# Cross-covariance attention: two heads per gram product, fp32 transposes into the gram banks, 512-byte buffers and a new order

## The chip, the cores and the metric

The kernel runs on one NeuronCore of one Trainium2 chip. The metric is the device time of one execution in microseconds (us). Three timed executions of the kernel before gave 131.87, 131.96 and 134.25 us, median 131.96. One further execution was profiled; all durations below are from that one. The engines are named as the profile names them: PE is the matrix engine (PEld its weight loads), DVE the vector engine, ACT the scalar engine, POOL the GpSimd engine, SP the engine that issues nearly all DMAs.

## The reference

Eight batches of twelve heads, 96 heads in all, each with Q, K and V of 512 x 64 in fp32. The attention is between the 64 channels, not between the 512 positions:

```python
Q_norm = Q / (np.linalg.norm(Q, axis=-2, keepdims=True) + 1e-10)
K_norm = K / (np.linalg.norm(K, axis=-2, keepdims=True) + 1e-10)
attn = np.einsum('bhnd,bhne->bhde', Q_norm, K_norm)
attn = np.exp(attn - np.max(attn, axis=-1, keepdims=True))
attn = attn / (np.sum(attn, axis=-1, keepdims=True) + 1e-10)
return np.einsum('bhnd,bhde->bhne', V, attn)
```

Each of Q, K, V and the output is 12.58 MB, so 37.75 MB are read and 12.58 MB written.

## The kernel before, in words

The 96 heads are worked in S = 12 units of eight heads: four partition groups of 32 (h), and in each two heads (r). Two neighbouring units share one V block (w, six of them), which comes as two loads. For each unit s:

- `load_qk` (line 215) loads Q and K, 1 MB each, into one of six buffers; units named in `FINE` (0 and 1) load in halves of 512 KB. `load_v` (231) loads V into one of three buffers.
- `cast_k` (246) and `mask_q` (251) cast K and Q to bf16 (through the helper `copy`, lines 209, 211 and 213 for ACT, DVE and POOL). `square` (263) squares them: on DVE from the bf16 tile (271), on ACT from the fp32 tile (268).
- `grams` (273, product in line 282) forms K^T Q. One product takes one head and two of its time slices t, t+1 side by side, so the two 64x64 diagonal blocks of its 128x128 result are two halves of one head's gram, still to be added; a unit has 64 of them, with 32 partitions each. They land in a PSUM tile of four banks, one bank for each h.
- `sums` (291, line 297) adds the squares over partitions, eight products in a unit; `fold` (300) reduces the rest on DVE; `norms` (304, line 307) brings the sums onto partitions with two products, one for the upper and one for the lower 64 partitions; `powers` (309) makes 1/norm by Ln and Exp on ACT.
- `scale_k` (315, line 319) multiplies the gram by K's factors, in two DVE operations on 64 partitions each. `logits` (325, line 327) multiplies the scaled gram with `eye2`, two identities stacked: that adds the two halves and transposes at once; an fp32 product is two instructions in the trace, so eight for a unit. It writes to the bank `l` (pool `ps_l`, one buffer) that sums and norms use too.
- `scales_q` (329, line 331), `exps` (333), `normalise` (337; z in line 339, rinv 341, rb 343, ab 346) finish the softmax; the result `ab` is block-diagonal bf16 for two heads.
- `cast_v` writes V as bf16 pairs, `vtrans` (359) transposes them on PE, `vcopy` brings them to SBUF as `vt`, `outs` (374) multiplies with `ab` into `po`, `ocopy` copies `po` to `so`, and `store` (235) writes 1 MB. Unit S - 3 is stored in four pieces by partitions (`CUTS`, line 240).

Each of these is a piece of work with a guessed cost for each engine that may do it, the pieces that it must follow (`after`), the pieces that it may not overtake (`behind`) and a rank. A planner, `Order.run` (100), places the pieces in a model of the engines, one at a time, and the kernel is then emitted in that order: each engine has a fixed list, and SP's list of loads and stores is fixed as well. For casts, squares, V casts and the two kinds of copies (`CHOICE`, 434) the planner also picks the engine: the one with the lowest model end plus a `BIAS` for that kind and engine. `R` holds the ranks. `NB` has the numbers of buffers. What holds a buffer back is in lines 451 to 482: a Q or K load waits for the cast and the square of the unit that had the buffer (`uses`, 452); `gr` waits for both `kx` of the unit before (478); `s1` waits for `qs` of the unit before (481).

SBUF tiles are allotted in the order in which their pools are opened. The pool `const` is opened first, with two tiles `front0` and `front1` of 64 bytes that nothing uses; from the sizes of its tiles, the Q/K buffers and all large buffers behind them start 448 bytes past a multiple of 512.

Of the kernel before, what the change touches and what calls it, by code (L numbers as in the profile page):

```python
# [13 lines left out]
PAR = {'NB': {'qk': 6, 'v': 3, 'vb': 2, 'qm': 3, 'sq': 1, 'vt': 2, 'so': 7, 'sm': 2, 'ab': 4},  # L14
 'TAIL': 3,
 'FINE': (0, 1),
 'LONG': (),
 'BOTH': 4,
 'ACTQ': True,
 'X': 1.27,  # L20
 'R': {'ck': 1.3207,
       'q': 6.2518,
       'sq': -0.5047,
       'sk': 3.7122,
       'gr': 1.845,
       's1': -1.9166,
       'rd': -3.4497,
       'nn': 4.2104,
       'pw': -2.4263,
       'kx': 0.7415,  # L30
       'lg': -4.357,
       'qs': 2.8064,
       'ex': -3.2847,
       'nm': 0.8664,
       'cv': 1.7734,
       'vt': -1.4345,
       'vc': 8.5873,
       'ou': 6.3652,
       'oc': 0.5305},
 'BIAS': {('cv', 'DVE'): 1.4481,  # L40
          ('vc', 'ACT'): 0.7387,
          ('oc', 'DVE'): 0.1673,
          ('q0', 'ACT'): -2.0331,
          ('sk', 'ACT'): 0.1695,
          ('ck', 'DVE'): -0.7752,
          ('ck', 'ACT'): 3.4068,
          ('ck', 'POOL'): 0.1916,
          ('q0', 'DVE'): 1.3494,
          ('q0', 'POOL'): 1.3168,
          ('sq', 'DVE'): 0.5356,  # L50
          ('sq', 'ACT'): 0.3766,
          ('sk', 'DVE'): -1.1633,
          ('cv', 'ACT'): -0.4971,
          ('cv', 'POOL'): 0.2974,
          ('vc', 'DVE'): 0.9359,
          ('oc', 'ACT'): -0.8803},
 'QK_PACE': 1.1686,
 'V_FROM': 0.1368,
 'V_PACE': 1.8786,
 'ST_LAG': 2.2074,  # L60
# [11 lines left out]
class Order:  # L72
    HOP = 0.10
# [78 lines left out]
def kernel(  # L152
# [13 lines left out]
    FINE, LONG = PAR["FINE"], PAR["LONG"]  # L166
    BOTH = S - PAR["BOTH"]

    Qf, Kf = (x.rearrange("b h (p t) d -> (b h p) (t d)", t=TT).rearrange("(w r e p) x -> w e p r x", r=2, e=2, p=128)
              for x in (Q, K))  # L170
    Qs, Ks = (x.rearrange("b h (p t) d -> (b h p) (t d)", t=T).rearrange("(w r e p) x -> w e p r x", r=2, e=2, p=64)
# [7 lines left out]
    const = ctx.enter_context(tc.tile_pool(name="const", bufs=1))  # L179
# [7 lines left out]
    abp = ctx.enter_context(tc.tile_pool(name="abp", bufs=NB["ab"]))  # L187
    small = ctx.enter_context(tc.tile_pool(name="small", bufs=NB["sm"]))
# [13 lines left out]
    qk32, kb, qm, sq, v32, vb, gram, st, s2, nn, r12, kqs, lg, ls, ex, ab, vps, vt, po, so = ({} for _ in range(20))  # L202
# [12 lines left out]
    def load_qk(s, x, c):  # L215
        w, e = divmod(s, 2)
        if (s, x) not in qk32:
            qk32[s, x] = qp.tile([128, T, D], F32, name="qk32")
        issue = nc.scalar if (s, x) == (0, 1) and PAR["ACTQ"] else nc.sync
        o = qk32[s, x][:, cols(c)].rearrange("p t d -> p (t d)")  # L220
        if s not in LONG:
            i = (Qf, Kf)[x][w, e]
            if c is None:
                issue.dma_start(out=o.rearrange("p (r x) -> p r x", r=2), in_=i)
            else:
                issue.dma_start(out=o, in_=i[:, c])
            return
        for r in range(2):
            issue.dma_start(out=o[r::2], in_=(Qs, Ks)[x][w, e, :, r, cols(c).start * D:cols(c).stop * D])
# [16 lines left out]
    def cast_k(eng, s, c):  # L246
        if s not in kb:
            kb[s] = qmp.tile([128, T, D], BF16, name="kb")
        copy(eng, kb[s][:, cols(c)], qk32[s, 1][:, cols(c)])

    def mask_q(eng, s, n, c):
        if s not in qm:
            qm[s] = qmp.tile([128, 2, T, D] if s in LONG else [128, T, D], BF16, name="qm")
        if s not in LONG:
            copy(eng, qm[s][:, cols(c)], qk32[s, 0][:, cols(c)])
            return
        o, i, m = qm[s][:, n, cols(c)], qk32[s, 0][:, cols(c)], par[:, n:n + 1]
        if eng == "ACT":
            nc.scalar.activation(o, i, AF.Copy, scale=m)
        else:  # L260
            (nc.vector if eng == "DVE" else nc.gpsimd).tensor_scalar(out=o, in0=i, scalar1=m, scalar2=0.0, op0=ALU.mult, op1=ALU.add)

    def square(eng, s, x, c):
        if s not in sq:
            sq[s] = sqp.tile([128, 2, T, D], BF16, name="sq")
        o = sq[s][:, x, cols(c)]
        if eng == "ACT":
            nc.scalar.activation(o, qk32[s, x][:, cols(c)], AF.Square)  # L268
        else:
            i = (kb if x else qm)[s][:, cols(c)]  # L270
            nc.vector.tensor_tensor(out=o, in0=i, in1=i, op=ALU.mult)  # L271

    def grams(s, c):
        if s not in gram:
            gram[s] = ps_g.tile([128, HU, 2, 2, 2 * D], F32, name="gram")
        if s not in LONG:
            for r in range(2) if c is None else (c,):
                for t in range(0, TT, 2):
                    for h in range(HU):
                        p = slice(32 * h, 32 * (h + 1))  # L280
                        k, q = (y[s][p, TT * r + t:TT * r + t + 2].rearrange("p t d -> p (t d)") for y in (kb, qm))
                        nc.tensor.matmul(gram[s][:, h, 0, r], k, q, start=(t == 0), stop=(t == TT - 2))  # L282
            return
        for t in range(cols(c).start, cols(c).stop, 2):
            for h in range(HU):
                p = slice(32 * h, 32 * (h + 1))
                nc.tensor.matmul(gram[s][:, h, 0].rearrange("p r d -> p (r d)"),
                                 kb[s][p, t:t + 2].rearrange("p t d -> p (t d)"),
                                 qm[s][p, :, t:t + 2].rearrange("p r t d -> p r (t d)"), start=(t == 0), stop=(t == T - 2))

    def sums(s, c):
        if s not in st:
            st[s] = ps_l.tile([D, 8, D], F32, name="l")
        for t in range(cols(c).start, cols(c).stop, 8):
            for x in range(2):
                m = hm[:, 0] if s in LONG else hm[:, 1 + t // TT]
                nc.tensor.matmul(st[s][32 * x:32 * (x + 1)].rearrange("p t d -> p (t d)"), m,  # L297
                                 sq[s][:, x, t:t + 8].rearrange("p t d -> p (t d)"), start=(t == 0), stop=(t == T - 8))

    def fold(s):  # L300
        s2[s] = small.tile([D, D], F32, name="s2")
        nc.vector.tensor_reduce(out=s2[s], in_=st[s].rearrange("p t d -> p d t"), axis=mybir.AxisListType.X, op=ALU.add)  # L302

    def norms(s):
        nn[s] = ps_l.tile([128, 12], F32, name="l")
        for i, half in enumerate((LO, HI)):
            nc.tensor.matmul(nn[s][half], s2[s], sel[:, i], start=True, stop=True)

    def powers(s):
        ln = small.tile([128, 12], F32, name="ln")  # L310
        r12[s] = small.tile([128, 12], F32, name="r12")
# [3 lines left out]
    def scale_k(s, n):  # L315
        if n == 0:
            kqs[s] = small.tile([128, 2 * HU, D], F32, name="kqs")
        half = (LO, HI)[n]
        nc.vector.tensor_tensor(  # L319
            out=kqs[s][half].rearrange("p (h r) d -> p h r d", r=2), in0=gram[s][half, :, 0, :, half],  # L320
            in1=r12[s][half, 0:2 * HU].rearrange("p (h r) -> p h r", r=2)[:, :, :, None].to_broadcast([D, HU, 2, D]), op=ALU.mult,
        )

    def logits(s):
        l = lg[s] = ps_l.tile([128, HU, D], F32, name="l")
        for h in range(HU):
            nc.tensor.matmul(l[:, h, :], kqs[s][:, 2 * h:2 * h + 2].rearrange("p r d -> p (r d)"), eye2, start=True, stop=True)  # L327

    def scales_q(s):
        ls[s] = small.tile([128, HU, D], F32, name="ls")  # L330
        nc.vector.tensor_tensor(out=ls[s], in0=lg[s], in1=r12[s][:, 8:12, None].to_broadcast([128, HU, D]), op=ALU.mult)  # L331
# [50 lines left out]
    pads = [const.tile([128, D // 4], F32, name=f"front{i}") for i in range(2)]  # L382
# [12 lines left out]
    par = const.tile([128, 2], F32, name="par")  # L395
    nc.vector.tensor_reduce(out=par, in_=ident.rearrange("p (i r) -> p r i", r=2), axis=mybir.AxisListType.X, op=ALU.add)
    hm = const.tile([128, 3, 32], BF16, name="hm")
    nc.gpsimd.memset(hm, 0.0)
    head = const.tile([128, HU, 2], F32, name="head")
    nc.vector.tensor_reduce(out=head, in_=ident.rearrange("p (h i r) -> p h r i", h=HU, r=2), axis=mybir.AxisListType.X, op=ALU.add)  # L400
    nc.vector.tensor_copy(hm[:, 0, 0:2 * HU], head.rearrange("p h r -> p (h r)"))
    own = const.tile([128, HU], F32, name="own")
    nc.vector.tensor_reduce(out=own, in_=ident.rearrange("p (h i) -> p h i", h=HU), axis=mybir.AxisListType.X, op=ALU.add)
    for r in range(2):
        nc.vector.tensor_copy(hm[:, 1 + r, r:2 * HU:2], own)
# [166 lines left out]
```

## Time and profile before

| what | value |
|---|---|
| median of three executions | 131.96 us (131.87 to 134.25) |
| the profiled execution | 130.95 us |
| its span, first to last instruction | 129.2 us |
| outside the span | 1.75 us |
| busy: DVE, ACT, PE, POOL | 94.7, 96.6, 84.3, 15.1 us |
| DMA | 50.59 MB in 11,633 packets |
| first and last data packet, from the span's start | 1.76 and 127.88 us |

The profile's page gives the busy time of each engine, then the span in 40 slices with the busy share of each engine in tenths, the clock granted to PE, and the busy share and rate of the 16 DMA engines that a core has. A group's row has line, engine, operation, the tiles written and read, shapes and count, then busy time and mean ns of one, then the idle time of the engine just before these instructions and what ended it. The view by stretches gives these for chosen windows.

### The profile page before, as it was taken

To read this page: it belongs to the slowest core of one execution; us is meant where nothing else is said; L and a number is where in the kernel's file an instruction comes from. 1 tells how busy PE (TensorE), PEld (TensorE's weight loads), DVE (VectorE), ACT (ScalarE), POOL (GpSimd) and SP (SyncE) were. 2 spreads that over 40 slices of the span, in tenths; PEclk is the share of its full clock that TensorE was granted. 3 is DMA by queue.
4 is the path that set the end of the run, shared out by engine and by line. 5 is a ranking of instruction groups with operands and counts; after the bars stand their busy time and mean duration, and the time that the engine had idled before them with its cause. 6 is when DMAs were issued, how large, how long until landed. Compare 5 with 4: busy or idle time off the path is not lost.

```text
span 129.2 us, 4217 instructions
## 1 busy us (share of the span) xinstructions
PE 84.3 (65%) x1872; PEld 59.0 (46%) x1872; DVE 94.7 (73%) x151; ACT 96.6 (75%) x134; POOL 15.1 (12%) x21
## 2 busy tenths in 40 slices
PE   0066197397767793995998968678549968776000
PEld 0022172274645552854846546346338555564000
DVE  3077747989989989688668999999997799751000
ACT  3333973595979999979749999999799689789200
POOL 5000500000710060514000001204000000000000
PEclk9999999959999999677569999999995999999755
DMA  4999999999999999999999999999999999997990
GB/s 131 417 419 417 412 410 410 413 424 411 405 410 413 405 419 405 421 398 420 430 402 405 415 427 405 419 406 422 402 419 421 413 410 416 413 397 271 389 392 32
DMA packets 11633, 50.59 MB, mean 392 GB/s; under 512 B 864, under 2 KB 864, under 8 KB 10080
## 3 DMA queue, kind: packets, MB, share of 16 engines
q1 hardware_dynamic: 11328, 49.29, 94.7%
q10 hardware_dynamic: 288, 1.05, 2.1%
q8 instruction: 14, 0.23, 0.7%
q14 instruction: 3, 0.02, 0.0%
HBM read 37.75 MB, written 12.58 MB: 390 GB/s over the span
## 4 chain that ended last, share of the span: by engine, by line
DVE 33%; PE 31%; ACT 20%; DMA 5%; issue 2%; SPq 0%; ACTq 0%
DVE kqs L319 10%; PE l L327 9%; DVE sq L271 9%; PE gram L282 9%; PE l L297 8%; DMA qk<-in_Q_dram 5%; DVE kb L211 5%; ACT vb L209 5%; ACT so L209 5%; PE vps L359 4%; ACT qm L209 4%; DVE s L302 3%; ACT vt L209 3%; DVE ab L346 2%; ACT sq L268 1%
## 5 line engine op out<-in xcount | busy, mean ns | idle before, releaser
L209 ACT CAST qm<-qk 128x2048 bf16<-128x2048 f32 (+1 forms) x14 | 23.2, 1656 | 4.5 <-DMA qk<-in_Q_dram 4.5
L209 ACT COPY so<-po 128x512 f32<-128x512 f32 x47 | 25.8, 590 | 1.0 <-PE po L374 0.9
L374 PE MATMUL po<-ab,vt 128*32 128x128 bf16 x768 | 21.7, 224 | 6.7 <-ACT so L209 6.1
L282 PE MATMUL gram<-qm,kb 32*128 32x128 bf16 x768 | 18.2, 261 | 8.5 <-DVE kb L211 8.5
L213 POOL TENSOR_SCALAR vb<-v 128x1024 bf16<-128x1024 f32 x8 | 13.5, 1682 | 74.7 <-DMA v<-in_V_dram 65.7
L327 PE MATMUL l<-eye,kqs 128*128 128x64 f32 x96 | 15.5, 314 | 9.7 <-DVE kqs L319 9.6
L209 ACT CAST vb<-v 128x1024 bf16<-128x1024 f32 x16 | 20.9, 1342 | 1.1 <-DMA v<-in_V_dram 1.1
L282 PEld LDWEIGHTS <-kb 32*128 32x128 bf16 x768 | 15.0, 116 | 11.8 <-DVE kb L211 9.4
L297 PE MATMUL l<-sq,hm 128*32 128x512 bf16 x96 | 18.2, 466 | 2.8 <-DVE sq L271 2.0
L359 PE MATMUL vps<-ident,vb 128*128 128x128 f32 x96 | 15.9, 292 | 5.2 <-ACT vt L209 2.3
L374 PEld LDWEIGHTS <-vt 128*32 128x32 bf16 x768 | 13.6, 96 | 12.3 <-issue 11.6
L327 PEld LDWEIGHTS l<-eye,kqs 128*128 128x128 f32 x96 | 13.9, 222 | 11.3 <-DVE kqs L319 3.5
L271 DVE TENSOR_TENSOR sq<-kb 128x2048 bf16<-128x2048 bf16 (+1 forms) x14 | 17.9, 1281 | 0.2
L209 ACT COPY vt<-vps 128x1024 bf16<-128x1024 bf16 (+1 forms) x15 | 14.3, 962 | 4.9 <-PE vps L359 4.9
L319 DVE TENSOR_TENSOR kqs<-gram,r 64x512 f32<-64x512 f32 x24 | 16.5, 686 | 2.0 <-ACT r L313 1.8
L359 PEld LDWEIGHTS vps<-ident,vb 128*128 128x128 f32 x96 | 11.0, 150 | 9.9 <-issue 3.9
L211 DVE CAST kb<-qk 128x2048 bf16<-128x2048 f32 (+1 forms) x14 | 14.9, 1067 | 0.2
L271 DVE TENSOR_TENSOR sq<-qm 128x2048 bf16<-128x2048 bf16 (+1 forms) x9 | 9.9, 1096 | 4.6 <-ACT qm L209 4.6
L302 DVE TENSOR_REDUCE s<-l 64x64 f32<-64x512 f32 x12 | 8.1, 679 | 4.3 <-PE l L297 4.2
L268 ACT ACTIVATE sq<-qk 128x2048 bf16<-128x2048 f32 (+1 forms) x5 | 7.8, 1568 | 3.7 <-PE l L297 3.7
L297 PEld LDWEIGHTS <-hm 128*32 128x32 bf16 x96 | 4.6, 104 | 9.5 <-issue 7.4
L331 DVE TENSOR_TENSOR ls<-l,r 128x256 f32<-128x256 f32 x12 | 5.1, 424 | 5.2 <-PE l L327 4.9
(29 smaller groups left out, 46.8 us busy)
## 6 DMA issues: line engine op xcount, KB each, us to landing
v<-in_V_dram SPq DMA_DIRECT2D x12, 1024.0 KB, 19.0
out_dram<-so SPq DMA_DIRECT2D x11, 1024.0 KB, 19.1
qk<-in_Q_dram SPq DMA_DIRECT2D x10, 1024.0 KB, 19.7
qk<-in_K_dram SPq DMA_DIRECT2D x10, 1024.0 KB, 19.8
qk<-in_Q_dram SPq DMA_DIRECT2D x4, 512.0 KB, 7.3
qk<-in_K_dram ACTq DMA_DIRECT2D x2, 512.0 KB
qk<-in_K_dram SPq DMA_DIRECT2D x2, 512.0 KB, 9.6
out_dram<-so SPq DMA_DIRECT2D x1, 512.0 KB, 5.6
```

The costliest lines, as they stand in the source:

```text
L209: nc.scalar.copy(o, i)
L211: nc.vector.tensor_copy(o, i)
L213: nc.gpsimd.tensor_scalar(out=o, in0=i, scalar1=1.0, scalar2=0.0, op0=ALU.mult, op1=ALU.add)
L268: nc.scalar.activation(o, qk32[s, x][:, cols(c)], AF.Square)
L271: nc.vector.tensor_tensor(out=o, in0=i, in1=i, op=ALU.mult)
L282: nc.tensor.matmul(gram[s][:, h, 0, r], k, q, start=(t == 0), stop=(t == TT - 2))
L297: nc.tensor.matmul(st[s][32 * x:32 * (x + 1)].rearrange("p t d -> p (t d)"), m, sq[s][:, x, t:t + 8].rearrange("p t d -> p (t d)"), start= ...
L302: nc.vector.tensor_reduce(out=s2[s], in_=st[s].rearrange("p t d -> p d t"), axis=mybir.AxisListType.X, op=ALU.add)
L319: nc.vector.tensor_tensor(out=kqs[s][half].rearrange("p (h r) d -> p h r d", r=2), in0=gram[s][half, :, 0, :, half], in1=r12[s][half, 0:2 ...
L327: nc.tensor.matmul(l[:, h, :], kqs[s][:, 2 * h:2 * h + 2].rearrange("p r d -> p (r d)"), eye2, start=True, stop=True)
L359: nc.tensor.transpose(ps[:, n], vb[w][:, j].rearrange("p r d c -> p (r d c)").bitcast(F32), ident)
L374: nc.tensor.matmul(po[s, x][32 * h:32 * (h + 1), j].rearrange("p r d -> p (r d)"), v, ab[s][:, h].rearrange("p r d -> p (r d)"), start=Tru ...
```

## The change

- **Layout of the casts.** `cast_qk` replaces `cast_k` and `mask_q`: the bf16 tiles hold, for each time slice, the two heads r side by side (`[128, TT, 2, D]`). The squares, on both engines, now read the bf16 tile, so a Q or K buffer is free after its cast.
- **Grams.** One product takes one time slice of two heads; 64 in a unit as before, with the same shapes, but the two diagonal blocks of a result are now the grams of two heads, complete after sixteen slices. They are issued for a whole unit, not for half of one.
- **Norms.** `s2` is 64 x 128, and one product with `sel` gives all eight factors.
- **Scaling, turning, scaling.** `scale_k` is one DVE operation on 128 x 512. `logits` are four fp32 transposes of 128 x 128 into the second quarter of each gram bank. `scales_q` is two DVE operations on 64 partitions, each reading its diagonal block there. `gr` of the next unit therefore waits for both `qs`; `s1` waits only for `pw`.
- **Buffers.** Q/K buffers 6 to 7, bf16 Q and K 3 to 2, squares 1 to 2, `so` 7 to 6. A first pool `edge` with a tile of 384 bytes, behind 128 bytes of built-in constants, puts all the large buffers at multiples of 512 bytes; `const` moves behind them.
- **Order.** New ranks, biases, paces and costs for the planner; unit 1 is no longer loaded in halves. The constants `par`, `head`, `eye2` go, and code for a second layout (`LONG`) that was not in use.

```diff
-PAR = {'NB': {'qk': 6, 'v': 3, 'vb': 2, 'qm': 3, 'sq': 1, 'vt': 2, 'so': 7, 'sm': 2, 'ab': 4},
+PAR = {'NB': {'qk': 7, 'v': 3, 'vb': 2, 'qm': 2, 'sq': 2, 'vt': 2, 'so': 6, 'sm': 2, 'ab': 4},
- 'FINE': (0, 1),
+ 'FINE': (0,),
...
+ 'BIAS': {('cv', 'DVE'): 12.3272,
+          ('vc', 'ACT'): 5.2627,
+          ('oc', 'DVE'): 7.9654,
+          ('q0', 'ACT'): -9.0842,
+          ('sk', 'ACT'): 4.174,
+          ('sk', 'DVE'): 5.4091,
+          ('cv', 'ACT'): 0.906,
+          ('cv', 'POOL'): -0.1651,
+          ('ck', 'DVE'): -11.8527,
+          ('ck', 'ACT'): -10.4645,
+          ('ck', 'POOL'): -15.4937,
+          ('oc', 'ACT'): 4.7795,
+          ('sq', 'DVE'): -12.3114,
+          ('sq', 'ACT'): -21.9953,
+          ('q0', 'DVE'): -28.6804,
+          ('q0', 'POOL'): -29.3142,
+          ('vc', 'DVE'): -20.4676},
- 'QK_PACE': 1.1686,
- 'V_FROM': 0.1368,
- 'V_PACE': 1.8786,
- 'ST_LAG': 2.2074,
+ 'QK_PACE': 0.9356,
+ 'V_FROM': 0.0874,
+ 'V_PACE': 0.7666,
+ 'ST_LAG': 6.0835,
...
-    HOP = 0.10
+    HOP = 0.06
...
+    def cast_qk(eng, s, x, c):
+        if (s, x) not in qkb:
+            qkb[s, x] = qmp.tile([128, TT, 2, D], BF16, name="qb" if x == 0 else "kb")
+        copy(eng, qkb[s, x][:, :, heads(c)], qk32[s, x][:, cols(c)].rearrange("p (r t) d -> p t r d", t=TT))
...
+    def grams(s):
+        gram[s] = ps_g.tile([128, HU, 4, 2 * D], F32, name="gram")
+        for t in range(TT):
             for h in range(HU):
+                q, k = (qkb[s, x][32 * h:32 * (h + 1), t].rearrange("p r d -> p (r d)") for x in range(2))
+                nc.tensor.matmul(gram[s][:, h, 0], k, q, start=(t == 0), stop=(t == TT - 1))
...
+        nn[s] = ps_l.tile([128, 2 * HU], F32, name="l")
+        nc.tensor.matmul(nn[s], s2[s], sel, start=True, stop=True)
...
+        nc.vector.tensor_tensor(out=kqs[s], in0=gram[s][:, :, 0], in1=r12[s][:, HU:, None].to_broadcast([128, HU, 2 * D]), op=ALU.mult)
...
-            nc.tensor.matmul(l[:, h, :], kqs[s][:, 2 * h:2 * h + 2].rearrange("p r d -> p (r d)"), eye2, start=True, stop=True)
+            nc.tensor.transpose(gram[s][:, h, 1], kqs[s][:, h], ident)
...
+        nc.vector.tensor_tensor(out=ls[s][half], in0=gram[s][half, :, 1, half], in1=r12[s][half, :HU, None].to_broadcast([D, HU, D]), op=ALU.mult)
...
-    pads = [const.tile([128, D // 4], F32, name=f"front{i}") for i in range(2)]
+    pad = edge.tile([128, 96], F32, name="pad")
+    nc.gpsimd.memset(pad[:1], 0.0)
...
-        return [] if i < 0 else every("ck", s) + every("sk", s) if x else every("q0", s) + (every("q1", s) if s in LONG else []) + every("sq", s)
+        return every("ck" if x else "q0", s)
```

## The prediction

> **What bounds the kernel now.** I read the slices first, then the same span in four stretches, then SP's own waits and the DMA issues, and last the rows of the groups that the change touches. The 40 slices:
>
> ```profile
> DVE  3077747989989989688668999999997799751000
> ACT  3333973595979999979749999999799689789200
> DMA  4999999999999999999999999999999999997990
> GB/s 131 417 419 417 412 410 410 413 424 411 405 410 413 405 419 405 421 398 420 430 402 405 415 427 405 419 406 422 402 419 421 413 410 416 413 397 271 389 392 32
> ```
>
> The DMA row stands at 9 from the second slice to slice 36 and the rate stays near 413 GB/s. DVE and ACT have slices at 5 to 8 in between. In four stretches (busy us of each engine, granted clock, DMA share, rate):
>
> ```profile
> 0.00:10.00 10.00, 2.01 (x36) 0.91 (x36) 4.13 (x12) 3.86 (x4) 1.65 (x13) 1.00 0.84 328
> 10.00:110.00 100.00, 74.90 (x1632) 52.56 (x1632) 85.82 (x131) 83.54 (x113) 13.46 (x8) 0.91 1.02 413
> 110.00:120.00 10.00, 7.42 (x204) 5.52 (x204) 4.70 (x10) 8.78 (x19) 0.00 (x0) 1.00 0.94 357
> 120.00:129.00 9.00, 0.00 (x0) 0.00 (x0) 0.00 (x0) 0.39 (x1) 0.00 (x0) 0.57 0.68 274
> ```
>
> Put together: the 50.59 MB at 413 GB/s take 122.5 us. The first packet starts at 1.76. Up to 10 us, (413 - 328)/413 x 10 = 2.06 us are short, 0.30 more than that start. From 110 to 120, (413 - 357)/413 x 10 = 1.36 us are short. From 120 on, 274 x 9 = 2.47 MB would need 5.97 us and the last packet ends at 127.88: 1.91 us short, because some DMA engines end later than others. 1.76 + 122.5 + 0.30 + 1.36 + 1.91 = 127.8, the end of the last packet. To that come 1.3 us to the span's end and 1.75 outside it: 130.95, the profiled execution's own time. So the transfers bound it; what work on the engines can win is the gap of 1.36, and perhaps the uneven end. SP's waits say who made the gap, the DMA issues how far the loads run ahead:
>
> ```profile
> SPq L242 <- ACT ex L335: 9.0, 2, 6.8
> ...
> SPq L240 <- ACT so L209: 6.5, 1, 6.5
> ...
> v<-in_V_dram SPq DMA_DIRECT2D x12, 1024.0 KB, 19.0
> out_dram<-so SPq DMA_DIRECT2D x11, 1024.0 KB, 19.1
> qk<-in_Q_dram SPq DMA_DIRECT2D x10, 1024.0 KB, 19.7
> ```
>
> The stores of the last units waited for the softmax and the output copies: the two longest waits, 6.8 and 6.5 us, stand just before the stores issued at 107.47 and 114.40. Everywhere else a transfer is issued some 19 us ahead of landing, so a late engine empties no DMA queue until that lead is gone.
>
> **The change part by part.** Rows that price it:
>
> ```profile
> L319 DVE TENSOR_TENSOR kqs<-gram,r 64x512 f32<-64x512 f32 x24 | 16.5, 686 | 2.0 <-ACT r L313 1.8
> L327 PE MATMUL l<-eye,kqs 128*128 128x64 f32 x96 | 15.5, 314 | 9.7 <-DVE kqs L319 9.6
> L359 PE MATMUL vps<-ident,vb 128*128 128x128 f32 x96 | 15.9, 292 | 5.2 <-ACT vt L209 2.3
> L331 DVE TENSOR_TENSOR ls<-l,r 128x256 f32<-128x256 f32 x12 | 5.1, 424 | 5.2 <-PE l L327 4.9
> ...
> 45.12 2.32 POOL L213 TENSOR_SCALAR vb<-v 128x1024 bf16<-128x1024 f32 x1 [9.07 <-PE vps L359]
> 80.30 1.35 POOL L213 TENSOR_SCALAR vb<-v 128x1024 bf16<-128x1024 f32 x1 [20.62 <-DMA v<-in_V_dram]
> ...
> 80.42 2.25 DVE L271 TENSOR_TENSOR sq<-kb 128x2048 bf16<-128x2048 bf16 x1
> ```
>
> Chain of one unit. Scaling: two operations of 0.69 us become one with as many elements per partition, -0.69. Turning: the eight instructions took 1.10 us at 113.16; four fp32 transposes in the `vps` row's form took 0.66 at 110.25: -0.44. Scaling by Q's factors: one of 0.42 becomes two on half the partitions; the operations on 64 and on 128 partitions cost by elements per partition (0.69 for 512, 0.42 for 256), so +0.42. Norm products: 48 instructions of 217 ns become 24; four took 0.29, two perhaps 0.2: -0.1. Together -0.8 us. Grams, sums and fold keep count and shape: nothing.
>
> Grams wait longer: `gr` of the next unit now waits for both `qs`, not for `kx`, so it starts later by 0.66 + 0.85 + some 0.1 less the 0.69 saved, 0.9 us, and PE's list behind it (sums, V's transposes, output products) with it; the casts and copies wait for those. Taken as nothing: PE is busy 65%, and the 19 us lead hides it. With no cover it would be 12 x 0.9 = 11 us.
>
> Engines. The biases in the diff say who gets what. K's cast: POOL's bias is 3.6 under DVE's and its cost 1.2 over, so POOL unless it is free 2.4 us later. Q's cast: 0.6 under and 1.2 over, so POOL when DVE is held up 0.6 us longer, and never ACT (19 over). Q's squares: ACT; V's copies from PSUM: DVE. From the busy rows, DVE: 94.7 - 8.2 (scaling) + 5.1 (Q's factors) - 9.9 (Q's squares) - 14.9 (K's casts) + 15 x 0.69 (V's copies) = 77 with Q's casts on POOL, 92 with them on DVE (12 x 1.22). ACT: 96.6 - 23.2 (Q's casts) - 14.3 (V's copies) + 24 x 1.9 - 7.8 (all squares) = 97 at most. Both fit into the 111 us from the first cast at 5.3 to the last output products. POOL's casts of K, 128x2048, are twice 1.35 us, about 2.7.
>
> POOL beside DVE: at 80.3 a POOL cast of 1.35 was running when a DVE square began: that took 2.25 us in place of 1.21. At 45.1 DVE had begun first and the POOL cast took 2.32. Three of eight POOL casts lengthened a square, by 3.0 us in all, 0.37 per cast; for casts twice as long, 24 x 0.75 = 18 us on DVE at most at that share: 95 us, still inside 111. Taken as nothing. The Trainium skill, SBUF: State Buffer, section Who interferes with whom, says that of a GpSimd instruction that reads SBUF and a DVE one with two SBUF inputs, or a cast, the second blocks fully until the first ends; by that, the trace agrees, and each of the new POOL casts could cost DVE up to its whole length.
>
> Loads and stores. Q/K buffers are freed after the cast, not after a square, and there are seven: loads can be issued earlier, worth nothing while the queue is full. Two DMAs fewer (unit 1 whole). The order of V, Q/K and stores in SP's list changes: V is asked for earlier and stores rank last, with six `so` buffers. A store that waits holds all loads behind it in SP's list; the 19 us hide 6.8. Unit 0's grams start only when both halves are cast (10.5 instead of 7.7): the first store is at 42.5, hidden. Fewer constants, one more fill on POOL: before the first data at 5.3, nothing.
>
> Buffers at multiples of 512 bytes: no row shows an aligned buffer. Packet records: of 9,216 packets of 4,096 bytes 5,023 took 159 ns, and 8,192 take 309 at the least, so 4,096 more bytes cost 150 and a packet 9 ns beside its bytes. Stores read SBUF at the odd offset and loads only write there, yet both have the floor of 159; and two instruction packets of 8,192 bytes took 309 and 311, like V's. That speaks for a cost that the offset doesn't set: 0. Ends: all 9 ns gone, 10,752 x 9/16 = -6.0 us; and, loads being mostly at 162 to 164 in midstream and stores at 159, +5 ns on 3,072 stores, +1.0 us.
>
> The gap of 1.36: it closes if the last stores are ready earlier. Units 10 and 11 are both finished after the last loads; each chain is 0.8 shorter, 1.6 in all, so I take all of it, -1.36; the ends are -1.36 and, if the new order makes the last store as late again, +1.4. Uneven end: `CUTS` is unchanged, 0 (ends -1.9 and +1.9).
>
> Sum: 130.95 - 1.36 = 129.6 for an execution like the profiled one. That one stood 1.0 under the median of the timed runs, 131.96; the prediction for a median is 129.6 + 1.0 = **130.6**, 1% under before. Within 2% is about what a measurement of this kernel can tell from no change.
>
> **The rivals.**
> - *The offset did cost transfer time.* If half or more of the 9 ns goes, the time is 130.6 - 3.0 = 127.6 or less, to 124.6. For it: all packets touch SBUF at an offset that the change removes, and loads and stores alike show the 9 ns. Against: the instruction packets. The Trainium skill, DMA: Bandwidth & Descriptors, section How a descriptor splits into AXI transactions, says that a transaction must start at a multiple of 256 bytes and bytes fetched ahead of the start cost beats. By that an estimate is six beats of 32 bytes at 150/128 ns each, 7 ns for each store, 1.4 us in all for stores; that loads, aligned in HBM, have the same floor is against it, unless writing costs likewise.
> - *Both tail losses go*: also the uneven 1.9, if the order leaves the DMA engines level: 128.7. Against: the store cut by partitions is the same.
> - *POOL blocks DVE* (slower). 24 casts of 2.7 are 65 us; DVE has 111 - 77 = 34 to spare. From 34 us blocked it decides; at 60%, 39 us, DVE ends 5 late: 135.6. For it: the 2.25 and 2.32 above. Against: only 3 of 8 met so far, and the planner keeps such pairs apart in its model.
> - *A store early in SP's list starves the loads*: a wait of 6.8 again, but with the lead half used: about +3, 133.6. Against: seven buffers, shorter chains.
>
> **How the numbers follow.** Forecast 0.60, offset 0.17, both tails 0.08, POOL 0.08, starved loads 0.07. The forecast's own range is 129.2 to 132 (gap open, 1.0 for slower stores, straggling). Faster by over 2% (under 129.3): 0.17 + 0.08 + 0.03 of the forecast's low edge = 0.28. Slower (over 134.6): POOL's 0.08 + 0.02 of starved loads = 0.10. Within: 0.62. The range 127.0 to 133.6 leaves out the deeper half of the offset case and the POOL case.
>
> **What would show it.** Scaling as twelve rows of 0.69; 48 transposes of about 0.29, four in 0.66; 24 of 0.42 for Q's factors; rate near 413 in the middle; 110 to 120 back at 413. The offset rival shows as 4,096-byte packets under 157 ns and a middle rate over 420; POOL as DVE casts and squares over 2 us in numbers and DMA slices under 9 in the middle; starved loads as such slices after a long SP wait. A middle rate that moves by more than 2% either way, or DMA slices under 9 before 110 us, would make the prediction wrong.

## The result

The changed kernel takes 129.67 us (median of four executions, 129.58 to 129.97), the kernel before 131.92 (four, 131.41 to 134.25). The ratio is 0.985, with a 95% interval from 0.981 to 0.988: 1.5% faster, where 1% was forecast. The profiled execution took 129.72 us with a span of 127.6.

The slices of the profile after:

```profile
DVE  2223344899836988889886699985699976600000
ACT  4076658794698826998798988839479757880000
POOL 3250665460545196054518805442516400000000
...
DMA  4999999999999999999999999999999999999950
GB/s 117 412 419 437 421 414 437 408 420 416 429 420 429 419 420 408 421 415 428 407 434 415 416 419 420 428 414 416 430 419 416 414 417 414 415 416 406 408 234 15
```

The DMA row is at 9 from the second slice to slice 38; the hole of 271 GB/s that the kernel before had is gone. POOL, nearly idle before, now has work in most slices up to slice 32. The four stretches after:

```profile
0.00:10.00 10.00, 0.17 (x8) 0.17 (x12) 2.03 (x5) 4.38 (x5) 3.98 (x13) 1.00 0.83 320
10.00:110.00 100.00, 77.46 (x1690) 51.79 (x1686) 77.63 (x134) 76.41 (x105) 43.04 (x27) 0.90 1.02 420
110.00:120.00 10.00, 3.22 (x114) 2.00 (x113) 0.69 (x2) 4.33 (x8) 0.00 (x0) 0.84 1.03 413
120.00:127.60 7.60, 0.00 (x0) 0.00 (x0) 0.00 (x0) 0.00 (x0) 0.00 (x0) 0.50 0.41 167
```

The same account as in the prediction, with the last packet ending at 126.18 us in place of 127.88:

| term | before | after | difference |
|---|---|---|---|
| 50.59 MB at the middle rate (413, 420 GB/s) | 122.5 | 120.45 | -2.05 |
| slow start beyond the first packet at 1.76 | 0.30 | 0.62 | +0.3 |
| gap from 110 to 120 us | 1.36 | 0.17 | -1.2 |
| uneven end, from 120 us on (3.02 us of work up to 126.18) | 1.91 | 3.16 | +1.25 |
| end of the last packet | 127.88 | 126.18 | -1.7 |

So the gap closed, as forecast. But the end became more uneven by as much as the gap gave (+1.25 against -1.2), and what is left of the gain is the rate, which was not forecast. The packets' own durations give the same size: the 9,216 packets of 4,096 bytes took 163.5 ns on average before and 160.9 after, the 1,536 of 8,192 bytes 315.7 and 309.6; spread over 16 engines that is 1.5 and 0.6 us. The groups that the change touches, after:

```profile
L209 POOL TENSOR_SCALAR kb<-qk 128x2048 bf16<-128x2048 f32 x11 | 20.9, 1901 | 32.6 <-DMA qk<-in_K_dram 24.8 <-PE gram L289 3.1 <-PE l L266 3.1
L207 DVE CAST qb<-qk 128x2048 bf16<-128x2048 f32 x10 | 12.3, 1226 | 5.0 <-DMA qk<-in_Q_dram 4.2 <-PE po L338 0.7
L295 DVE TENSOR_TENSOR ls<-gram,r 64x256 f32<-64x256 f32 x24 | 10.1, 420 | 2.7 <-PE gram L289 2.3
L289 PE MATMUL gram<-ident,kqs 128*128 128x128 f32 x48 | 9.7, 335 | 4.0 <-DVE kqs L285 3.7
L285 DVE TENSOR_TENSOR kqs<-gram,r 128x512 f32<-128x512 f32 x12 | 8.3, 688 | 3.4 <-ACT r L281 2.9 <-issue 0.5
L275 PE MATMUL l<-sel,s 64*128 64x8 f32 x24 | 5.4, 294 | 4.4 <-DVE s L271 4.4
```

One scaling of 0.69 us for a unit; two of 0.42 for Q's factors; four transposes, 9.7/12 = 0.81 us for a unit where the eight instructions took 15.5/12 = 1.29. The norm products cost more than before, not less: 24 take 5.4 us, where 48 of half the width took 3.6. K's casts are POOL's, at 1.90 us.

### The profile page after: what moved, and what is told of

Same layout as the page of the kernel before. It is cut to its first block, busy times and chain, and to the rows that moved or that the text cites. A ratio compares the mean times of both kernels' runs of the same rounds, so it can differ in the third digit from the quotient of the medians.

```text
span 127.6 us, 4062 instructions
## 1 busy us (share of the span) xinstructions
PE 80.8 (63%) x1800; PEld 54.0 (42%) x1800; DVE 80.4 (63%) x140; ACT 85.1 (67%) x116; POOL 47.0 (37%) x40
## 2 busy tenths in 40 slices
DMA packets 11601, 50.59 MB, mean 396 GB/s; under 512 B 832, under 2 KB 832, under 8 KB 10048
## 4 chain that ended last, share of the span: by engine, by line
DMA 53%; PE 13%; DVE 12%; ACT 7%; SPq 4%; issue 2%
DMA qk<-in_Q_dram 36%; DMA v<-in_V_dram 17%; ACT so L205 4%; PE po L338 3%; SPq L225 3%; PE gram L289 3%; PE vps L323 3%; DVE ab L310 2%; PE l L266 2%; DVE vt L207 2%; PE gram L260 1%; DVE s L271 1%; ACT sq L251 1%; DVE sq L253 1%; ACT vb L205 1%
## 5 line engine op out<-in xcount | busy, mean ns | idle before, releaser
L209 POOL TENSOR_SCALAR kb<-qk 128x2048 bf16<-128x2048 f32 (+1 forms) x13 | 23.7, 1820 | 37.8 <-DMA qk<-in_K_dram 30.0
L251 ACT ACTIVATE sq<-qb 128x2048 bf16<-128x2048 bf16 (+1 forms) x13 | 23.1, 1778 | 8.2 <-DVE qb L207 8.2
L209 POOL TENSOR_SCALAR vb<-v 128x1024 bf16<-128x1024 f32 x15 | 20.3, 1372 | 13.5 <-DMA v<-in_V_dram 9.8
L260 PE MATMUL gram<-qb,kb 32*128 32x128 bf16 x768 | 15.3, 238 | 12.7 <-POOL kb L209 10.1
L207 DVE CAST qb<-qk 128x2048 bf16<-128x2048 f32 (+1 forms) x12 | 13.6, 1137 | 10.3 <-DMA qk<-in_Q_dram 9.5
L207 DVE COPY vt<-vps 128x1024 bf16<-128x1024 bf16 (+1 forms) x25 | 16.5, 665 | 3.0 <-PE vps L323 2.7
L251 ACT ACTIVATE sq<-kb 128x2048 bf16<-128x2048 bf16 (+1 forms) x10 | 17.4, 1737 | 0.6 <-POOL kb L209 0.6
L205 ACT CAST vb<-v 128x1024 bf16<-128x1024 f32 x9 | 12.0, 1338 | 6.8 <-DMA v<-in_V_dram 6.8
L289 PE MATMUL gram<-ident,kqs 128*128 128x128 f32 x48 | 9.7, 335 | 4.0 <-DVE kqs L285 3.7
L295 DVE TENSOR_TENSOR ls<-gram,r 64x256 f32<-64x256 f32 x24 | 10.1, 420 | 2.7 <-PE gram L289 2.3
L310 DVE TENSOR_TENSOR ab<-ex,rb 128x512 bf16<-128x512 f32 x12 | 10.4, 867 | 0.4
```

The lines of the kernel that those rows point to most:

```text
L205: nc.scalar.copy(o, i)
L207: nc.vector.tensor_copy(o, i)
L209: nc.gpsimd.tensor_scalar(out=o, in0=i, scalar1=1.0, scalar2=0.0, op0=ALU.mult, op1=ALU.add)
L251: nc.scalar.activation(o, i, AF.Square)
L260: nc.tensor.matmul(gram[s][:, h, 0], k, q, start=(t == 0), stop=(t == TT - 1))
L289: nc.tensor.transpose(gram[s][:, h, 1], kqs[s][:, h], ident)
```

## Experiments

Three questions were open: what raised the rate, what closed the gap, and what made the end more uneven. All ratios are to the kernel before, run on the same chip.

**The rate.** Theory A: the offset of the buffers sets how long packets take. Theory B: the other order and engine work do.

`e1_after_off448`:

```diff
-    pad = edge.tile([128, 96], F32, name="pad")
+    pad = edge.tile([128, 80], F32, name="pad")
```

> The changed kernel, with its first tile 64 bytes shorter, so that all large buffers start 448 bytes past a multiple of 512, as before the change. Theory A (the start of the buffers sets how long load packets take): load packets of 4,096 bytes go back to 160 to 169 ns, the rate from 10 to 110 us from 420 to about 413 GB/s, and the time from 129.7 to about 131.5 us. Theory B (the other order and the other engine work made the packets shorter): packets stay at 159, the rate at 420, the time at 129.7.

Measured: 131.51 us, ratio 1.0005 (0.996 to 1.005). The middle and end stretches of this kernel:

```profile
10.00:110.00 100.00, 77.04 (x1652) 51.26 (x1642) 75.37 (x132) 75.01 (x102) 43.07 (x27) 0.90 1.02 413
110.00:120.00 10.00, 4.41 (x160) 2.79 (x148) 2.05 (x4) 5.47 (x10) 0.00 (x0) 0.88 0.98 386
```

413 again, with the new order and all the new engine work: theory B is out. Without the offset the change wins nothing that can be measured, although the gap is only (413 - 386)/413 x 10 = 0.65 us here. The last packet ends at 127.66 us, and the uneven end, by the same account, is 2.35 us in place of the 1.91 of before.

`e3_after_off256` (the same tile with 160 columns) and `e10_after_off128` (with 128 columns) ask for the unit.

> The changed kernel with all large buffers 256 bytes past a multiple of 512. Theory A with 256 bytes as the unit: like the changed kernel, 159 ns, 420 GB/s, 129.7 us. Theory A with 512 as the unit: load packets over 159, about 413 GB/s and 131.5 us. Theory B: like the changed kernel.

> The changed kernel with all large buffers 128 bytes past a multiple of 512. If a packet's target has to start at a multiple of 256: packets at 160 to 169, 413 GB/s, 131.5 us. If 128 suffices: 159, 420, 129.7.

Measured: at 256 past, 129.70 us, ratio 0.987 (0.983 to 0.991); at 128 past, 131.34 (two executions), ratio 0.997 (0.986 to 1.007). Their middle stretches, 256 first:

```profile
10.00:110.00 100.00, 78.42 (x1700) 52.86 (x1696) 77.97 (x134) 77.15 (x106) 42.67 (x27) 0.85 1.02 420
```

```profile
10.00:110.00 100.00, 75.19 (x1636) 50.09 (x1629) 74.74 (x132) 74.84 (x102) 43.94 (x27) 0.91 1.02 413
```

A multiple of 256 is enough, 128 is not. Then which buffers? `e6_after_loads_off448` moves only the targets of the loads, with a small tile behind them that brings the rest back; `e7_after_rest_off448` the rest alone:

```diff
     vp = ctx.enter_context(tc.tile_pool(name="vp", bufs=NB["v"]))
+    fill = ctx.enter_context(tc.tile_pool(name="fill", bufs=1))
...
-    pad = edge.tile([128, 96], F32, name="pad")
+    pad = edge.tile([128, 80], F32, name="pad")
     nc.gpsimd.memset(pad[:1], 0.0)
+    gap = fill.tile([128, 16], F32, name="gap")
+    nc.gpsimd.memset(gap[:1], 0.0)
```

(e7 keeps 96 and gives `gap` 112 columns.)

> The changed kernel with only the fp32 Q/K and V buffers, the targets of the loads, 448 bytes past a multiple of 512; everything behind them, the store buffers too, at multiples of 512. If it is the writing of the load packets: 4,096-byte packets of loads at 160 to 169, 413 GB/s, 131.5 us, as with all buffers off. If it is the engines' traffic to bf16 tiles and store buffers, or the stores: 159 ns, 420 GB/s, 129.7 us.

> The counterpart: load buffers at multiples of 512, all large buffers behind them (bf16 tiles, squares, V, store buffers) 448 bytes past. If it is the writing of the load packets: 159 ns, 420 GB/s, 129.7 us. A start rule for reads would show here: six more beats of 32 bytes in each store packet, some 7 ns (an estimate), so stores at 166 and 131.0 us.

Measured: loads off 131.81 us, ratio 0.999 (0.995 to 1.002); the rest off 130.01, ratio 0.985 (0.980 to 0.990). Middle stretches, loads off first and with the stretches behind it:

```profile
10.00:110.00 100.00, 78.85 (x1652) 52.03 (x1648) 76.40 (x132) 75.70 (x102) 43.29 (x27) 0.85 1.02 413
110.00:120.00 10.00, 4.66 (x164) 2.96 (x152) 1.79 (x4) 5.47 (x10) 0.00 (x0) 0.80 1.02 410
120.00:129.60 9.60, 0.00 (x0) 0.00 (x0) 0.00 (x0) 0.00 (x0) 0.00 (x0) 0.50 0.53 217
```

```profile
10.00:110.00 100.00, 78.25 (x1704) 51.99 (x1696) 78.21 (x134) 76.78 (x106) 42.59 (x27) 0.90 1.02 420
```

As far as the times can tell, the whole effect is in the load targets. The packet records say how, by the number of the 8,960 packets of 4,096 bytes in SP's queue that took 159 ns (the other 256, unit 0's K, go through ACT's queue):

| kernel | load targets | rest | at 159 ns | middle GB/s |
|---|---|---|---|---|
| before | 448 | 448 | 5,023 | 413 |
| after | 0 | 0 | 8,789 | 420 |
| e1 | 448 | 448 | 4,766 | 413 |
| e3 | 256 | 256 | 8,760 | 420 |
| e10 | 128 | 128 | 5,410 | 413 |
| e6 | 448 | 0 | 4,880 | 413 |
| e7 | 0 | 448 | 8,675 | 420 |

(offsets: bytes past a multiple of 512.) The floor of 159 ns is the same in all seven (at most 12 packets fall below it). With an odd target most of the others took 160 to 172 ns; with a target at a multiple of 256 nearly all packets are at the floor. Loads alone are seen from 15 to 40 us, before the first store: there 1,319 of 1,726 such packets took 160 to 175 ns in the kernel before, 1,254 of 1,727 in e6 and 2 of 1,772 in the changed kernel. Stores alone are seen from 116 us on: from an odd source 70 of 717 took 160 to 175 ns in e7, 4 of 702 in the changed kernel, so the source costs a little too.

The two kernels with odd load targets and the new order also price the gap:

| kernel | gap, 110 to 120 us | uneven end | both |
|---|---|---|---|
| before | 1.36 | 1.91 | 3.27 |
| e1 | 0.65 | 2.35 | 3.00 |
| e6 (last packet at 128.16) | 0.07 | 3.12 | 3.19 |
| after | 0.17 | 3.16 | 3.33 |

What closing the gap gave came back as an uneven end, and e1 and e6 take as long as the kernel before. That fits DMA engines which end last and were not the ones that idled in the gap; the records do not name the engines, so this reason is not shown.

**The gap.** Is the offset alone worth the 2 us? `e2_before_off0`, run again as `e5_before_off0_again`:

```diff
-    pads = [const.tile([128, D // 4], F32, name=f"front{i}") for i in range(2)]
+    pads = [const.tile([128, D // 4], F32, name=f"front{i}") for i in range(3)]
```

> The kernel before, with a third unused tile of 64 bytes ahead, so that all large buffers start at multiples of 512. Theory A: load packets at 159 ns, a middle rate of 420 GB/s, 2 us of transfer less; since the last stores are not ready earlier, the gap between 110 and 120 us grows by up to the same 2 us, so the time lies between 130.0 and 131.9 us. Theory B: packets at 160 to 169, rate 413, time 131.9 as before.

> Once more the kernel before with all large buffers at multiples of 512, since its four executions lay from 129.8 to 134.2 us. Theory A2 (with transfers 2 us shorter the last units' compute is the bound at the end, so the end follows the compute): packets again at 159 ns, 420 GB/s from 10 to 110 us, a gap from 110 to 120 us well over the 1.36 us of before, and times that spread from 129.8 upwards. Rival (the spread was a disturbance of those executions): all executions near 129.8 us, the gap near 1.4 us.

Measured: the executions of this kernel lie far apart, 129.8 to 134.2 us in the first series and 129.3 to 135.3 (twelve, median 132.27) in the second, so its time is not compared and only its profile is read. Middle and next stretch of e2 (a long execution, of 133.01 us):

```profile
10.00:110.00 100.00, 78.96 (x1560) 55.68 (x1564) 81.47 (x126) 80.23 (x110) 13.29 (x8) 0.86 1.02 420
110.00:120.00 10.00, 7.67 (x212) 5.79 (x201) 7.67 (x16) 8.82 (x16) 0.00 (x0) 1.00 0.68 243
```

The rate is 420, and the gap is (420 - 243)/420 x 10 = 4.2 us: in this execution the transfers wait for the last units' work. In the one of e5, of 135.29 us, the rate is 420 as well and the gap 4.5 us. A few executions did gain; most did not. No profile of one near 129.8 us was taken, so whether its gap was smaller is not shown. In most executions the offset alone gains nothing.

`e9_after_old_order` keeps all of the change, the new costs in the planner's model too, except the ranks, biases and paces (all of `R`, `BIAS` and the four paces; shortened here):

```diff
- 'R': {'ck': 14.3601,
-       'q': -46.9145,
...
+ 'R': {'ck': 1.3207,
+       'q': 6.2518,
...
- 'QK_PACE': 0.9356,
- 'V_FROM': 0.0874,
- 'V_PACE': 0.7666,
- 'ST_LAG': 6.0835,
+ 'QK_PACE': 1.1686,
+ 'V_FROM': 0.1368,
+ 'V_PACE': 1.8786,
+ 'ST_LAG': 2.2074,
```

> The changed kernel with the ranks, biases and paces of the kernel before, all else changed (products, transposes, buffers at multiples of 512, numbers of buffers, costs). If the shorter chain suffices: no gap, 129.5 to 130.5 us. If the new order (POOL for K's casts, V earlier) is what makes the last stores early: a gap between 110 and 120 us again, 131 us or more.

Measured: 130.77 us, ratio 0.992 (0.986 to 0.999).

```profile
10.00:110.00 100.00, 73.45 (x1580) 49.45 (x1584) 87.79 (x140) 76.18 (x107) 14.13 (x8) 0.84 1.02 419
110.00:120.00 10.00, 8.91 (x208) 6.12 (x208) 3.10 (x5) 7.58 (x13) 1.37 (x1) 0.71 0.85 301
```

With the old order DVE has 88 of the middle 100 us instead of 78, POOL 14 instead of 43, and a gap of 2.8 us is there. So the new products do not close the gap by themselves; the new order, which hands K's casts to POOL among other things, is part of it. Which of its parts counts was not separated.

`e8_after_chain_longer` puts more on each unit's chain than the change took off; `e11_after_kx_two` has its first edit alone, `e12_after_transposes_twice` its second:

```diff
-        nc.vector.tensor_tensor(out=kqs[s], in0=gram[s][:, :, 0], in1=r12[s][:, HU:, None].to_broadcast([128, HU, 2 * D]), op=ALU.mult)
+        for half in (LO, HI):
+            nc.vector.tensor_tensor(out=kqs[s][half], in0=gram[s][half, :, 0], in1=r12[s][half, HU:, None].to_broadcast([D, HU, 2 * D]), op=ALU.mult)
...
-        for h in range(HU):
+        for h in [*range(HU), *range(HU)]:
             nc.tensor.transpose(gram[s][:, h, 1], kqs[s][:, h], ident)
```

> The changed kernel with the scaling by K's factors as two operations on 64 partitions, as before, and the four transposes done twice (the second time for nothing). That puts 0.69 + 0.66 = 1.35 us back on each unit's chain, more than the 0.8 that the prediction took from it. If the shorter chain closed the gap of 1.36 us between 110 and 120 us, it opens again: rate there under 390 GB/s and 130.5 to 131.5 us. If the new order closed it (the last stores are issued well ahead), 129.7 us and about 413 GB/s stay.

> The changed kernel with only the scaling by K's factors as two DVE operations on 64 partitions (0.69 us more on each unit's chain, 8.3 us more on DVE). Chain theory (each unit's chain adds up over the twelve units and the lists of the engines pass it on to the last stores): a large part of 8.3 us less the some 2 us by which the last store's data trail its issue, so 133 to 137 us, with the DMA slices full up to about 100 us and a gap behind. Slack theory (one such step fits into the lead, and the jump to 144 us came from both steps together): under 131 us.

> The changed kernel with only the four transposes of each unit done twice (0.66 us more on the chain, 7.9 us more on PE, nothing on DVE). Chain theory: as with the two scalings, 133 to 137 us. If DVE's list, with what POOL holds up on it, is what runs out of slack and not the chain: 129.7 to 131 us here, and 133 or more with the two scalings.

Measured: both 144.37 us (ratio 1.089, 1.079 to 1.099); the two scalings alone 140.49, with executions from 134.56 to 140.84, too far apart for a ratio; the transposes twice 130.18 (ratio 0.988, 0.982 to 0.993), about as the changed kernel. e8 is far outside what either theory gave, and most executions of e11 above the 133 to 137 of the chain theory. Where e8's time went is in its slices:

```profile
DMA  4999999999999999999999999999993007638892
GB/s 134 395 422 436 412 421 424 418 423 430 411 424 421 419 417 421 424 411 432 420 412 418 432 412 413 435 415 412 421 415 131 0 5 299 256 155 251 309 416 99
```

For 30 slices nothing shows; the transfers run on at some 420. Then everything that had fallen behind, unit by unit, is missing at once: the stores have nothing to store, and one of SP's two waits for the output copies lasts 22.6 us. In e11 the store of unit 6 is issued at 113.65 us; in the changed kernel that is 97.18. The transposes on PE add (15.0 - 9.7)/12 = 0.44 us to each unit and cost next to nothing. The 0.69 on DVE cost eleven in most executions. That speaks for DVE's list as what ran out, and not the chain as such; but the step on PE was also the smaller one, and a chain with room for 0.44 us and not for 0.69 is not ruled out. DVE's rows of e11 (the execution of 140.65 us) show what became longer:

```profile
L207 DVE CAST qb<-qk 128x2048 bf16<-128x2048 f32 x10 | 18.3, 1832 | 2.6 <-DMA qk<-in_Q_dram 2.0 <-PE gram L260 0.6
L286 DVE TENSOR_TENSOR kqs<-gram,r 64x512 f32<-64x512 f32 x24 | 16.5, 686 | 4.2 <-ACT r L281 2.8 <-PE gram L260 1.2
...
L308 DVE TENSOR_TENSOR rb<-rinv,side 128x8 f32<-128x8 f32 x12 | 5.3, 440 | 0.4
```

Beside the 8.2 us of the second scaling, Q's casts take 1.83 us in place of 1.23, and `rb`, an operation on eight columns, 0.44 in place of 0.23 on average. POOL's casts of K rose from 1.90 to 2.18. e8 has the same, casts of 1.79 and `rb` of 0.68. The lists of POOL and DVE are fixed; shifted against each other, operations meet that the order had kept apart, and one holds up the other (a pair from e8 is shown at the end). Over the shortest of its kind, DVE's casts and its operations on two tiles were lengthened by 4.6 us in all in the changed kernel, by 12.9 in e11 and by 13.5 in e8. That the holding up is the whole of the rest, and not also the waits between the shifted lists, was not separated.

**The end.** `e4_after_whole_store`:

```diff
-        if s == S - PAR["SPLIT"]:
+        if False:
```

> The changed kernel with unit 9 stored whole, as the other units are, not in four pieces by partitions. The last packet of the changed kernel ends at 126.2 us, while half of the DMA engines have ended by 123.5. If the late engine is one of those that get the long piece of 85 partitions, the end comes 1 to 2 us earlier (128 to 128.7 us); if it is one of those that the pieces relieve, about 0.9 us later (130.6 us).

Measured: 128.21 us, ratio 0.976 (0.972 to 0.979), the best of all kernels run. Its last stretch:

```profile
120.00:127.00 7.00, 0.00 (x0) 0.00 (x0) 0.00 (x0) 0.00 (x0) 0.00 (x0) 0.50 0.46 188
```

The last packet ends at 124.69 in place of 126.18. In the changed kernel the completions of the last store come up to 124.6 us but for one at 126.18; with the whole store seven come from 124.4 to 124.7. So the pieces, left as they were, cost 1.5 us here: gap and uneven end together are 1.65 us with the whole store (0.10 and 1.55), 3.33 with the pieces. That the pieces gave their load to an engine that was late without them fits, but the records do not name the engines. Why some DMA engines are late at all was not tried, nor was the whole store in the kernel before.

## Why the prediction was right, and where it was not

The number was right, and partly by luck: the one term that was to bring the gain brought none, and a term that was taken as 0 brought it.

- **Transfers are the bound**: right. The DMA row is full up to 120 us, and the time follows the rate: 129.7 us at 420 GB/s (e3), 131.5 and 131.8 at 413 (e1, e6).
- **The gap of 1.36 closes**: right in size, 0.17 is left. The reason, a chain 0.8 us shorter, was only half right. The PE part of it is not needed (e12), with the DVE part put back the gap is far larger (e8, e11), and without the new order it does not close (e9: 2.8 us).
- **The gap is the gain, and the uneven end 0**: this step failed. The sum takes "-1.36" for the gap and "0" for the end as if one did not touch the other. The end grew by 1.25, and gap and end together went from 3.27 to 3.33. With the gap closed and the rate left at 413, e6 takes as long as the kernel before (ratio 0.999). The +1.25 lies inside the stated ends of 1.9, and e4 shows the pieces behind it.
- **Offset taken as 0**: wrong, it was -2.05 us, the whole of the gain. The step that failed: "That speaks for a cost that the offset doesn't set: 0". The rows were in hand: loads at 162 to 164 in midstream, stores at 159. I looked for the offset in the floor of 9 ns, which e1 to e7 show unmoved, and read the loads' excess as a loss that stores might share (+1.0), not as what an odd target costs. (The 5,023 packets at 159 ns are of the 8,960 in SP's queue, not of 9,216; nothing hangs on it.) The rival was right that the offset costs transfer time; its mechanism, a lower floor, was wrong, and the saving was below the 3.0 us from which it counted. The signs set for it came out at their edge: two packets under 157 ns, a rate of 420 and not over it. The move of the rate, 1.7%, was just under the 2% that would have made the prediction wrong. Of the Trainium skill's page DMA: Bandwidth & Descriptors, section How a descriptor splits into AXI transactions, the unit of 256 bytes agrees with e3 and e10. Its charge for an odd start on the reading side, an estimated 7 ns for each store packet, does not show in that form: with store buffers 448 past, 608 of the 717 packets from 116 us on stayed at 159 ns (e7). Most of the cost was on the writing side, in loads.
- **The 1.0 us from the profiled execution to a median**: there was none here. The profiled execution of the changed kernel took 129.72, its median is 129.67. The sum of 129.6 before this step lies nearer, but it is made of the gap's 1.36 and not of the rate's 2.05.
- **POOL beside DVE, taken as nothing**: right for this kernel, 4.6 us of lengthening against 3.8 before, with casts of 1.90 us and not 2.7. But a price of that size is real: e8 and most executions of e11 go past the rival's 135.6, with less than the 34 us of blocking from which it was to decide: 8.2 us of DVE work came with 8 us of added lengthening. The busy sum against 111 us did not show this, since in these runs the lists lost time long before DVE was full. The Trainium skill, SBUF — State Buffer, section Who interferes with whom, agrees with the rows that got longer: casts, and products with two inputs.
- **"The 19 us lead hides it"**: right until the lead is gone, and e8 shows what it means: a delay that repeats in each unit is not hidden by a lead, only shown later.
- **Norm products -0.1**: wrong sign, +0.15 us a unit (5.4 against 3.6 us in all), without visible effect.

## What to carry to other kernels

Put the targets of loads at multiples of 256 bytes and check it in the packet records: a spread of durations above a clean floor, in a stretch where only loads run, is the sign. A gap in the mean rate of all DMA engines need not be a gain: in e6 1.3 us of it closed, and the last packet came no earlier (128.16 us against 127.88). A faster transfer is kept only if the last stores are ready that much earlier, so read the work of the last units together with the rate. When an order is made anew, look again at what was balanced by hand at the end: the pieces of one store cost 1.5 us after the change.

## What the runs showed of the hardware that was not expected

- An odd target costs three in four load packets of 4,096 bytes between 1 and some 13 ns beyond 159 (before, 15 to 40 us: 1,319 of 1,726 took 160 to 175), and the others nothing. Packets of 8,192 bytes, V's, pay as well: 315.5 ns on average in that stretch, 309 in the changed kernel. An odd source costs about one store packet in ten as much (e7, from 116 us on: 70 of 717). 128 past a multiple of 256 is nearly as bad as 192 (e10: 1,129 of 1,749).
- How long a small DVE operation is held: `rb`, eight columns, takes 0.17 us at its shortest, and here, in the timeline of e8, 1.87, from just after POOL's cast began until that cast's end:

```profile
59.77 1.90 POOL L209 TENSOR_SCALAR kb<-qk 128x2048 bf16<-128x2048 f32 x1 [2.92 <-PE gram L260]
59.82 1.87 DVE L308 TENSOR_TENSOR rb<-rinv,side 128x8 f32<-128x8 f32 x1
```

- Halving the number of norm products did not save PE time: 48 instructions on half of the columns were busy 3.6 us, 24 on all of them 5.4.
